# Prompt scores from three rounded products of high and low parts, in place of plain fp32

## The chip, the core and the metric

The kernel runs on one core of a Trainium2 chip. TensorE (PE) multiplies matrices out of SBUF into PSUM; VectorE (DVE), ScalarE (ACT) and GpSimd (POOL) do the rest of the arithmetic; SyncE (SP) and POOL issue most of the DMAs. The metric is the device time of one execution in microseconds (us), the median of several runs. Smaller is better.

## The reference

One step of a hybrid network with two layers over 640 tokens: a prompt of 512 frames and 8 running streams of 16 frames each. A layer is a half-step feed-forward block (FFN), a mixer (a short convolution, attention, and gates that merge them), and a second half-step FFN. The change lies in the attention of the prompt: 8 heads of 64 channels, 64-frame chunks, each of which reads its own chunk and those before it, and a learned bias by relative distance:

```python
s = jnp.einsum('bqhd,bkhd->bhqk', q, k).astype(jnp.float32) * (HEAD_DIM ** -0.5)
...
s = s + rel_bias[:, idx].astype(jnp.float32)[None]
...
valid = (k_pos[None, :] >= 0) & (kc <= qc) & (kc >= qc - N_PREV_CHUNKS)
s = jnp.where(valid[None, None], s, NEG_INF)
p = jax.nn.softmax(s, axis=-1).astype(v.dtype)
return jnp.einsum('bhqk,bkhd->bqhd', p, v)
```

All inputs and outputs are fp32. The keys of the prompt and of the streams are outputs too.

## The kernel before

**Rounded products.** Nearly all matrix products are done in a rounded fp32 form (type `fp32r`). A number z is split into hi, z rounded to that form by a copy on ScalarE, and lo = z - hi, a subtraction on VectorE that writes the same form. A product is then hi·hi + hi·lo + lo·hi, three matmuls into one PSUM bank. Weights are split so as well while they stream in: `raw` is loaded on SP's queue (L292), ScalarE writes `whi` (L364), VectorE `wlo` (L369).

**Seven products for eight.** A pair of output tiles (q and k of two heads, for example) is made by `seven` (L833), a Strassen-like scheme with seven half products on four chunks of weights. It is a generator: between its blocks of six matmuls it yields, 14 times in all. Banks pa, pb and pc (in the profile `ma_qk`, `mb_qk`, `mc_qk`) are read by VectorE and ScalarE in the middle of a pair and at its end; TensorE goes on adding to pa and pc after some of these readings. `both` (L1377) gives the readings for a pair without a convolution: `up1` and `up2` write the first output, `lo2` the second half (columns 320 to 639) of the second output, and `lo1` its first half (columns 0 to 319), last of all. `third` and `last` are called behind `up2` and `lo1`.

**Queries and keys.** `qk(p)` (L1796) makes q and k of heads 2p and 2p+1 as tiles of 128 channels (64 for each head) by 640 tokens. `queries`, run as `third`, scales q on VectorE (L1802) and copies the streams' part to `bd` on POOL; `keys`, run as `last`, stores k (L1809, a DMA that POOL issues) and copies the streams' part to `ks`. q and k have two buffers each, of the pool `mp` (tags "q" and "k").

**Filling.** TensorE's order is written out by hand through the attention: `fill(n)` takes n steps (blocks of six matmuls) of the stream `work` (q and k of pairs 1 to 3, then convolution, gates) and puts them between the parts of the attention, so that TensorE has work while softmax runs. `scores(p)` (L1859) does the scores of two heads, `turn(p)` transposes the weights, `values(p)` multiplies them with v. VectorE, ScalarE, POOL and SP have no order written out there: a planner orders their instructions by when it thinks that they can run, and those under `soon()` come ahead of others.

**Scores.** In `scores(p)` the prompt has four row blocks i of 128 queries, with 128·(i+1) keys each, so 128, 256, 384 and 512 columns. For each block the two heads come one behind the other: channels 0 to 63 and 64 to 127, into two different PSUM banks. These are fp32 matmuls (L1882). VectorE adds the bias and takes the maximum (L1888), ScalarE does the exponentials (L2082) and scales them (L1899).

**After the prompt.** The streams' attention reads cached keys (`kc`, L1992, loaded on SP's queue) into buffers of the tags "q" and "k", that is, into those that q and k of the prompt leave. `tmp` gives a tile of 128 x 640 out of four shared temporaries; the convolution uses two at a time.

## Time and profile before

| | |
|---|---|
| median of 3 runs | 2481.96 us (2481.89 to 2482.2) |
| the profiled execution | 2481.95 us |
| its span, first to last instruction | 2480.2 us |
| TensorE busy | 2467.0 us, 17264 matmuls |
| VectorE busy | 2182.4 us |
| ScalarE busy | 1385.6 us |
| granted TensorE clock | 1.0 |

How the lines are read: a row of a group has the line of the kernel, the engine, the operation, output tile <- input tiles (buffer numbers left out), shapes (partitions x elements), the count, and behind it the busy time in us and the mean of one in ns, then the idle time of the engine just before them and who ended it. A row of the timeline has start and length in us. A matmul's shape is given as rows x columns of the array, then the moving operand. An fp32 matmul shows as two matmuls; rounded operands are shown as f32 in matmul rows. A matmul's length covers its way through the array, so matmuls overlap, and the rate is the distance of their starts. PEld is the loading of weights into the array.

### The profile page before, as it was taken

How to read it: one execution, taken by the hardware profiler on the slowest of the kernel's cores; microseconds unless marked ns; L12 is line 12 of the kernel's file. 1: busy time of each engine (PE TensorE's matmuls, PEld its weight loads, DVE VectorE, ACT ScalarE, POOL GpSimd, SP SyncE). 2: the span in 40 equal slices, each digit the busy share in tenths (PEclk: the TensorE clock that was granted, in tenths of full speed). 3: DMA queues.
4: the chain of work that ended last, by engine and by line, in shares of the span. 5: the costliest groups of instructions: out<-in, count | busy, mean ns of one | idle time of the engine just before them, and what ended most of it. 6: DMA issues, size and time to landing. Idle time of an engine off the chain costs nothing.

```text
span 2480.2 us, 44054 instructions
## 1 busy us (share of the span) xinstructions
PE 2467.0 (99%) x17264; PEld 2414.6 (97%) x17264; DVE 2182.4 (88%) x3643; ACT 1385.6 (56%) x2230; POOL 319.5 (13%) x483
## 2 busy tenths in 40 slices
PE   9999999999999999999999999999999999999999
PEld 8999999889999999999999999998899999999998
DVE  7999998888888899998799999988888889999997
ACT  6555556675555555555665555566655556555555
POOL 0111112211000001111001010121110000111111
PEclk9999999999999999999999999999999999999999
DMA  4443444335344334444334343452453333444444
GB/s 155 127 117 102 120 118 125 110 114 174 99 118 124 94 102 107 112 118 118 110 94 109 110 117 102 117 128 103 137 167 94 118 119 93 107 113 107 112 117 117
DMA packets 113520, 288.16 MB, mean 116 GB/s; under 512 B 12992, under 2 KB 52544, under 8 KB 113312
## 3 DMA queue, kind: packets, MB, share of 16 engines
q1 hardware_dynamic: 69552, 220.10, 27.0%
q0 software_dynamic: 43328, 64.99, 13.8%
q8 instruction: 135, 2.21, 0.4%
q14 instruction: 73, 0.60, 0.1%
q10 hardware_dynamic: 432, 0.25, 0.0%
HBM read 239.48 MB, written 7.94 MB: 100 GB/s over the span
## 4 chain that ended last, share of the span: by engine, by line
PE 93%; DVE 3%; ACT 2%; issue 1%; DMA 1%; SPq 0%; DVEq 0%; ACTq 0%; POOLq 0%
PE pab L459 12%; PE paa L459 11%; PE pcb L459 6%; PE daa L1144 6%; PE pca L459 5%; PE dab L1144 5%; PE po L435 5%; PE qa L459 4%; PE pbb L459 3%; PE dca L1144 3%; PE pba L459 3%; PE dcb L1144 2%; PE ma_cv L459 2%; PE ma_qk L459 2%; PE py L435 2%; PE pv L1835 2%
## 5 line engine op out<-in xcount | busy, mean ns | idle before, releaser
L364 ACT CAST whi<-raw 128x512 fp32r<-128x512 f32 (+1 forms) x577 | 501.7, 874 | 371.6 <-PE pbb L459 46.0
L369 DVE TENSOR_TENSOR wlo<-raw,whi 128x512 fp32r<-128x512 f32 (+1 forms) x577 | 577.1, 1002 | 137.1 <-ACT whi L364 132.9
L364 ACT CAST whi<-s 128x1024 fp32r<-128x1024 f32 (+1 forms) x162 | 152.8, 943 | 320.3 <-DVE s L296 113.9
L459 PE MATMUL pab<-xhib,whi 128*128 128x320 f32 x704 | 217.7, 309 | 0.0
L459 PE MATMUL pab<-xlob,whi 128*128 128x320 f32 x704 | 217.3, 309 | 0.0
L459 PE MATMUL pab<-xhib,wlo 128*128 128x320 f32 x704 | 217.3, 309 | 0.0
L459 PE MATMUL paa<-xhia,whi 128*128 128x320 f32 x640 | 197.8, 309 | 0.2 <-DVE ga L296 0.2
L459 PE MATMUL paa<-xhia,wlo 128*128 128x320 f32 x640 | 197.6, 309 | 0.0
L459 PE MATMUL paa<-xloa,whi 128*128 128x320 f32 x640 | 197.5, 309 | 0.0
L369 DVE TENSOR_TENSOR wlo<-s,whi 128x1024 fp32r<-128x1024 f32 (+1 forms) x162 | 176.4, 1089 | 4.4 <-ACT whi L364 4.4
L1166 POOL DMA_DIRECT2D x<-c_a x80 | 69.8, 1019 | 575.2 <-ACT ahia L1048 205.5
L1166 POOL DMA_DIRECT2D x<-c_b x72 | 63.1, 1011 | 583.2 <-ACT ahib L1048 205.4
L459 PEld LDWEIGHTS pab<-xhib,whi 128*128 128x128 f32 x704 | 132.1, 188 | 0.9 <-issue 0.9
L459 PEld LDWEIGHTS pab<-xlob,whi 128*128 128x128 f32 x704 | 132.1, 188 | 0.0
L459 PEld LDWEIGHTS pab<-xhib,wlo 128*128 128x128 f32 x704 | 132.1, 188 | 0.0
L459 PEld LDWEIGHTS paa<-xhia,whi 128*128 128x128 f32 x640 | 120.1, 188 | 1.1 <-DVE ga L296 0.5
L459 PEld LDWEIGHTS paa<-xloa,whi 128*128 128x128 f32 x640 | 120.1, 188 | 0.3 <-DVE xloa L703 0.3
L459 PEld LDWEIGHTS paa<-xhia,wlo 128*128 128x128 f32 x640 | 120.1, 188 | 0.2
L296 DVE TENSOR_TENSOR raw<-s,raw 128x512 f32<-128x512 f32 x162 | 110.8, 684 | 0.0
L459 PE MATMUL pcb<-xhib,wlo 128*128 128x320 f32 x352 | 108.9, 309 | 0.0
L459 PE MATMUL pcb<-xlob,whi 128*128 128x320 f32 x352 | 108.7, 309 | 0.0
L459 PE MATMUL pcb<-xhib,whi 128*128 128x320 f32 x352 | 108.7, 309 | 0.0
(909 smaller groups left out, 8200.5 us busy)
## 6 DMA issues: line engine op xcount, KB each, us to landing
raw<-in_wst SPq DMA_DIRECT2D x375, 512.0 KB, 3.6
x<-c_a POOLq DMA_DIRECT2D x80, 160.0 KB, 4.9
x<-c_b POOLq DMA_DIRECT2D x72, 160.0 KB, 4.2
lent<-in_wst POOLq DMA_DIRECT2D x36, 256.0 KB, 3.7
kc<-in_kcache SPq DMA_DIRECT2D x32, 256.0 KB, 4.9
vc<-in_vcache SPq DMA_DIRECT2D x16, 512.0 KB, 4.3
one<-in_wst POOLq DMA_DIRECT2D x32, 256.0 KB, 3.9
x<-u_a POOLq DMA_DIRECT2D x40, 160.0 KB, 4.1
```

The lines of the kernel that those rows point to most:

```text
L296: DVE.tensor_tensor(out=out, in0=a, in1=b, op=op)
L364: ACT.copy(hi[:, d], src[:, c])
L369: DVE.tensor_tensor(out=lo, in0=src, in1=hi.bitcast(F32), op=ALU.subtract)
L435: PE.matmul(ps[:, a, :HT], w, x[a] if isinstance(x, tuple) else x[:, a * HT : (a + 1) * HT], start=first and j == 0 and not seeded, stop=l ...
L459: PE.matmul(ps, a, b, start=start and kp == 0 and j == 0, stop=stop and kp == NP - 1 and j == 2, skip_group_check=True)
L1144: PE.matmul(ps[u], w, y, start=start and i == 0 and j == 0, stop=i == 1 and j == 2, skip_group_check=True)
L1166: POOL.dma_start(x[ms[2 * u + r]][:, cols], z[:, u], accum_op=ALU.add)
L1835: PE.matmul(pv[t], xx[:, t * P : (t + 1) * P], w[:, kk * AW : (kk + 1) * AW], start=c == 0 and kk == 0 and j == 0, stop=c == KT // 2 - 1 a ...
```

## The change

q and k of the prompt are no longer kept as they are for the scores. They are made in two of the shared temporaries, and for each of them a high and a low part of the prompt's 512 columns are written into the two buffers that q (or k) had: `parts` does a ScalarE copy and a VectorE subtraction, both under `soon()`. q is split in one piece of 512 columns behind its scaling. k is split in two: columns 320 to 511 in the middle of the pair (through the new argument `mid` of `both`), columns 0 to 319 at its end.

In `scores` each block is three rounded products (high·high, low·high, high·low), added up in one bank, and for each of the three the heads alternate. The matmuls still use 64 rows for each head.

The calls of `fill` are changed so that every `scores(p)` comes one step later in TensorE's order; `turn` and `values` stay at the step where they were.

```diff
-                def both(n, u, g, third, last, scale=-1.0):
+                def both(n, u, g, third, last, scale=-1.0, mid=None):
 
                     (up1, up2), (lo2, lo1) = upper(u), lower(g, scale)
+
+                    def half(pa):
+                        lo2(pa)
+                        if mid:
+                            mid()
...
-                    return pair(n, up1, lo2, end1, end2)
+                    return pair(n, up1, half, end1, end2)
...
-            q = qa[p] = mp.tile([P, T], F32, name=f"q{l}_{p}", tag="q")
-            k = ka[p] = mp.tile([P, T], F32, name=f"k{l}_{p}", tag="k")
+            q = tmp(f"q{l}_{p}")
+            k = tmp(f"k{l}_{p}")
+            qa[p], ka[p] = ([mp.tile([P, T], F32R, name=f"{z}{i}{l}_{p}", tag=z)[:, :SEQ]
+                             for i in ("hi", "lo")] for z in "qk")
+
+            def parts(zs, z, c):
+                hi, lo = (y[:, c] for y in zs)
+                with soon():
+                    ACT.copy(hi, z[:, c])
+                    DVE.tensor_tensor(out=lo, in0=z[:, c], in1=hi.bitcast(F32), op=ALU.subtract)
 
             def queries():
                 DVE.scalar_tensor_tensor(out=q, in0=q, scalar=HD ** -0.5, in1=rr, op0=ALU.mult, op1=ALU.mult)
+                parts(qa[p], q, slice(0, SEQ))
...
             def keys():
+                parts(ka[p], k, slice(0, HT))
                 POOL.dma_start(ko[l, :, p, :], k)
                 POOL.tensor_copy(ks[:, p, :], k[:, SEQ:])
 
-            return both(f"qk{p}", q, k, queries, keys)
+            return both(f"qk{p}", q, k, queries, keys, mid=lambda: parts(ka[p], k, slice(HT, SEQ)))
...
+                (qh, ql), (kh, kl) = qa[p], ka[p]
                 for i, c in spans:
-                    for e in range(2):
-                        r = slice(e * HD, (e + 1) * HD)
-                        PE.matmul(pss[e][:, c], qa[p][r, i * P : (i + 1) * P], ka[p][r, : (i + 1) * P],
-                                  start=True, stop=True)
+                    for j, (y, z) in enumerate(((qh, kh), (ql, kh), (qh, kl))):
+                        for e in range(2):
+                            r = slice(e * HD, (e + 1) * HD)
+                            PE.matmul(pss[e][:, c], y[r, i * P : (i + 1) * P], z[r, : (i + 1) * P],
+                                      start=j == 0, stop=j == 2)
...
-        fill(2)
+        fill(3)
         scores(0)
         fill(15)
         scores(1)
-        fill(4)
+        fill(3)
         turn(0, 0)
         fill(2)
         turn(0, 1)
         fill(2)
         values(0)
-        fill(6)
+        fill(7)
         scores(2)
         for p in range(1, npair):
             if p + 1 < npair:
-                fill(6)
+                fill(5)
                 turn(p)
-                fill(8 if p + 2 < npair else 11)
+                fill(9 if p + 2 < npair else 11)
                 values(p)
```

## The prediction

> **What bounds the kernel now.** I read the page first, then what TensorE waited for, then the chain of work that ended last, and only then the lines of the change.
>
> ```profile
> span 2480.2 us, 44054 instructions
> ...
> PE 2467.0 (99%) x17264; PEld 2414.6 (97%) x17264; DVE 2182.4 (88%) x3643; ACT 1385.6 (56%) x2230; POOL 319.5 (13%) x483
> ```
>
> ```profile
> PE poa L435 <- ACT whi L759: 5.3, 1, 5.3
> PE pca L459 <- DVE wlo L369: 0.5, 2, 0.3
> ```
>
> The profiled execution took 2481.95 us: its span of 2480.2 and 1.75 us around it. The median of the runs is 2481.96, so a sum against the profiled execution needs no correction. TensorE (PE) is busy for 99% of the span. Its longest wait in the whole kernel is the 5.3 us at the start, and no row of that list after the second is above 0.5. For the stretch from 440 to 560 us, which holds the attention of the first layer, the list is empty. So a microsecond taken off TensorE's own stream shows at the end, and work on VectorE (DVE) or ScalarE (ACT) costs nothing until TensorE has to wait for it.
>
> From the chain (start, length, what):
>
> ```profile
> 428.53 13.62 PE pv L1835 x60
> ...
> 471.48 2.36 PE pss L1882 x16
> ...
> 477.55 1.76 PE mc_qk L459 x12
> ...
> 514.80 2.18 PE ptp L1919 x20
> ...
> 2455.98 5.92 PE pdf L2197 x48
> ```
>
> and from the line of the scores:
>
> ```profile
> L1882 PE MATMUL pss<-k,q x128: 269/429/693, 471.4 to 1756.5; 64*128 64x512 f32 x32, 64*128 64x256 f32 x32, 64*128 64x128 f32 x32, 64*128 64x384 f32 x32
> ```
>
> The scores of one pair of heads (pss) are 16 matmuls in 2.36 us, and 128 / 16 makes eight such calls, four in each layer: 18.9 us in all. This is everything that the change can shorten, under 0.8% of the time.
>
> **Part 1: the products of the scores.** The 16 matmuls are two passes for each of eight fp32 products (four widths, two heads). From four narrow stretches of the first call, a row of each, and below them the loads of weights:
>
> ```profile
> 471.41 0.70 PE L1882 MATMUL pss<-k,q 64*128 64x512 f32 x2
> 471.94 1.03 PE L1882 MATMUL pss<-k,q 64*128 64x512 f32 x6
> 472.37 0.82 PE L1882 MATMUL pss<-k,q 64*128 64x256 f32 x8
> 472.80 1.03 PE L1882 MATMUL pss<-k,q 64*128 64x128 f32 x8
> ```
>
> ```profile
> 471.41 0.30 PEld L1882 LDWEIGHTS pss<-k,q 64*128 64x128 f32 x4 [0.19 <-issue]
> ```
>
> Two matmuls of up to 0.69 us lie within 0.70 from 471.41: the two heads already run beside each other, each in its 64 rows. The second pass over 512 columns lasts from 471.94 to 472.37, 0.43 us, and two passes over 256 from 472.37 to 472.80, 0.215 each. A pass moves 1.2 columns per ns, so a pair needs 2 x 1280 / 1.2 = 2.13 us; the other 0.23 of the 2.36 goes into changing to this mode and back (0.10 of it is seen in the first pass, which takes from 471.41 to 471.94).
>
> After the change each width has three rounded products. Rates of rounded products stand in the chain: 13.62 / 60 = 0.227 us for 512 columns, 1.76 / 12 = 0.147 for 320, 5.92 / 48 = 0.123 for 256. From 320 to 512 a column costs 0.42 ns, so 384 columns cost 0.174. For 128 rounded columns there is no row. Below, the line from 320 through 256 goes on to 0.075; above, the transposes of that width take 2.18 / 20 = 0.109. I take 0.109, the one row of that width. With the heads beside each other a pair costs 3 x (0.227 + 0.123 + 0.109 + 0.174) = 1.90 us, with the lower bound 1.80. That rounded halves run beside each other as the fp32 ones do is taken from these; no row shows it. The other end is one after the other, 3.80.
>
> Whether the 0.23 stays has no row either, since every small tile here is also fp32 and type and tile change together. Its bounds are 0 and 0.23; I keep 0.23, as the nearest row is this call's own. The new call is 1.90 + 0.23 = 2.13 in place of 2.36: 0.23 less, **1.9 us less in eight calls**. The Trainium skill, TensorEngine Tiling (Array Packing), Key Properties, says that changing the tiling mode drains the engine; by it the 0.23 stays, without it the call would be 1.90.
>
> The four loads of weights at 471.41 end within 0.30 us, while the first two matmuls run until 472.11. The third and fourth are for the same two halves, so a load goes on beside a matmul of its own half. The Trainium skill, TensorE: Matmul & The Clock Gate, The mechanism (Part 3), says that a load overlaps a matmul in flight only where the row group differs. The trace disagrees, for fp32; if it held for rounded products it would be the rival "loads" below.
>
> **Part 2: the rounded parts.** Each pair gets three copies on ScalarE (512, 320 and 192 columns) and three subtractions of these widths on VectorE.
>
> ```profile
> L369 DVE TENSOR_TENSOR wlo<-s,whi 128x512 fp32r<-128x512 f32 x6 | 4.2, 701 | 0.0
> ...
> L1368 DVE SCALAR_TENSOR_TENSOR k<-ma_qk,rrm 128x320 f32<-128x320 f32 x4 | 1.9, 484 | 0.0
> ```
>
> ```profile
> L364 ACT CAST whi<-s 128x512 fp32r<-128x512 f32 x6 | 3.7, 615 | 5.9 <-DVE s L296 5.8
> ...
> L863 ACT COPY c<-mc_qk 128x320 f32<-128x320 f32 x4 | 1.6, 412 | 0.0
> ```
>
> Busy time of PE, PEld, DVE, ACT, POOL in the whole attention of the first layer, and in one pair's stretch of it:
>
> ```profile
> 457.26:558.27 101.01, 101.01 (x701) 90.11 (x699) 81.99 (x193) 69.03 (x158) 17.16 (x42) 1.00 0.37 126
> ```
>
> ```profile
> 469.56:484.42 14.86, 14.86 (x102) 13.54 (x101) 12.37 (x34) 10.76 (x25) 3.11 (x8) 1.00 0.37 130
> ```
>
> With the 320 price as the upper end for 192, VectorE gets 0.70 + 0.48 + 0.48 = 1.66 us a pair and ScalarE 0.62 + 0.41 + 0.41 = 1.44; in eight pairs 13.3 and 11.5. In the 101.01 us VectorE is idle for 19.0 and ScalarE for 32.0, and four pairs need 6.6 and 5.8. In the pair's own stretch VectorE has 2.49 idle for its 1.66. The cover is TensorE's filling products, and on average it holds: cost 0. Were it gone, VectorE's 13.3 us would show.
>
> The average isn't all. A subtraction waits for its copy at the head of VectorE's queue; behind it stand the weights' subtractions, the taking out of the next banks, and the maxima of the softmax, on which TensorE waits. Two places are tight:
>
> ```profile
> 469.61 0.82 DVE L1802 SCALAR_TENSOR_TENSOR q<-q,rrm 128x640 f32<-128x640 f32 x1
> 470.35 0.48 DVE L1368 SCALAR_TENSOR_TENSOR k<-ma_qk,rrm 128x320 f32<-128x320 f32 x1
> ...
> 480.87 1.23 DVE L369 TENSOR_TENSOR wlo<-raw,whi 128x1024 fp32r<-128x1024 f32 x1 [2.49 <-ACT whi L364]
> 482.02 0.17 DVE L2085 RECIPROCAL st<-st 128x4 f32<-128x4 f32 x1
> 482.10 0.46 DVE L296 TENSOR_TENSOR k<-ma_qk,c 128x320 f32<-128x320 f32 x1
> ```
>
> ```profile
> 482.66 0.38 PE L459 MATMUL ma_qk<-thi,whi 128*128 128x320 f32 x1
> 482.87 0.31 PE L459 MATMUL ma_qk<-tlo,whi 128*128 128x320 f32 x1
> ```
>
> First, the start of the scores. Now q is ready at 470.43, k at 470.83, and the scores begin at 471.41. One filling step is half of the 1.76 us of twelve products, 0.88, so they would begin at 472.29. New in between: ScalarE copies q until 471.05 and k until 471.46; VectorE subtracts q until 471.75 and k until 472.23. k's low part is needed only after two products of 512 columns, 0.45 later. So the first call has about 0.5 us in hand, and the other three of a layer, which now have a step more, 0.88 more. Cost 0; one foreign operation of 0.62 or 0.70 us in front would use it up in the first call.
>
> Second, the product after a bank's middle reading. At 482.10 VectorE takes out k's half, behind a weight subtraction that itself waited 2.49 us for ScalarE, and TensorE's next product on that bank starts when it is done (482.66, 0.38 long in place of 0.31). There is nothing in hand there. ScalarE's softmax now comes 0.88 us later against the filling products and its queue is 1.44 us fuller, so this can get later or, with another order, earlier. Bounds: a gain of the 0.1 us that it costs now, a loss of one 512-column subtraction, 0.70, in each pair. I take 0.1 us more for each of the eight pairs, near the row, **0.8 us**.
>
> **Part 3: what moves with the scores and the tiles.** The scores, with the bias loads that POOL issues for the pair after, come one step later, and all later fills are adjusted so that transposes and values keep their places. Issue and need of a bias shift together: cost 0. q and k now live in the four shared temporaries; the convolution's tiles that follow take the buffers of pair 2, whose outgoing DMA is a whole pair (14 steps of 0.88) back: cost 0. Both buffers of a name now hold the high and low part of one pair, so the cached keys of the first sample batch, loaded on SP's queue into the same buffers, can start only when the last scores are done:
>
> ```profile
> 509.43 0.39 SPq L1992 DMA_DIRECT2D kc<-in_kcache  x1
> ...
> 528.85 0.38 SPq L1992 DMA_DIRECT2D kc<-in_kcache  x1
> ```
>
> ```profile
> L2005 PE MATMUL spss<-kc,bd x128: 392/392/417, 558.3 to 1839.5; 128*32 128x272 f32 x128
> ```
>
> They go from 509.43 to about 528.85 with the second batch's, and are first used at 558.3: cost 0. Weight loads stand on the same queue; if the order of that queue weren't adjusted, one of them would wait up to 19 us. POOL's copy of the new keys into these tiles waits for the same release.
>
> **Sum.** 2481.95 - 1.9 + 0.8 = 2480.85; I predict 2480.8.
>
> **The rivals.**
> - *The switch goes too.* If the 0.23 belongs to fp32 and not to the small tile, and 128 columns cost 0.075, a call is 1.80: 0.56 less, and the product behind it also loses its late start, about 0.1 by the 0.10 at the entry. 8 x 0.66 = 5.3 us: 2476.7. For it: no row separates type and tile. Against: it needs both bounds at once. With one of them it is 2478 to 2480.
> - *The queues get in the way.* One 0.70 us subtraction in front of TensorE in each pair: 2481.95 - 1.9 + 5.6 = 2485.7; a 1024-column one of 1.23 us: 2489.9. It decides once VectorE runs later than the 0.5 us in hand at the scores or the nothing at 482.66. For it: that row, and ScalarE 1.44 us fuller. Against: 19.0 us of idle in 101.
> - *Loads.* Every product pays for its load. A load of 128 columns is at most the 0.109 of a transpose; twelve a call, in front of their products: 1.80 + 12 x 0.109 + 0.23 = 3.34, 0.98 more, 2489.8. Against: the row of four loads. Nearly the same time comes out if a rounded 64-row tile runs no faster than fp32, so that the change doesn't do what it says: 3 x 1280 / 1.2 + 0.23 = 3.43, 2490.5.
> - *One head after the other.* 3.80 + 0.23 = 4.03 a call, 1.67 more: 2495.3. It decides if a rounded product holds all 128 rows. For it: no rounded product of 64 rows is in the trace. Against: the two fp32 halves at 471.41.
>
> **How the numbers follow.** Forecast 47%, its own range 2479 to 2482.5; the switch 18%; the queues 16%; loads or no faster 8%; one after the other (or a blocked weight load) 11%. About 0.2% is what a measurement of this kernel can tell from no change: below 2477.0 is faster, above 2486.9 slower. Faster holds 15 of the switch's 18; slower holds 9 of the queues', 8 and 11: 28; the rest, 57, is same. The range from 2476.5 to 2490 leaves out the last rival and a little at both ends.
>
> **What would show it.** A score call in the chain of 24 matmuls and about 2.13 us; two matmuls from one moment in its first stretch; three intervals near 0.23 us for 512 columns. Near 1.8 the switch went; near 3.4 it is loads or rate; near 4 the heads follow each other. Waits of TensorE for the new high and low parts, or longer first products behind a bank's reading, would show the queues. The prediction is wrong if pss rows keep 2.36 us or more with TensorE still at 99%.

## The result, and the profile after

The changed kernel takes **2487.64 us** (median of 13 runs, 2486.96 to 2488.61) against 2482.2 (median of 13 runs beside it, 2481.72 to 2482.68): a ratio of **1.0022, with an interval of 1.0013 to 1.003**. It is slower by 5.4 us where 1.2 us less was forecast. The profiled execution took 2488.61 us.

From the page of the changed kernel, its span, the busy times, and the shares by engine of the chain that ended last:

```profile
span 2486.8 us, 44241 instructions
...
PE 2468.2 (99%) x17328; PEld 2418.0 (97%) x17328; DVE 2192.3 (88%) x3667; ACT 1393.8 (56%) x2254; POOL 313.2 (13%) x483
...
PE 89%; DVE 5%; ACT 3%; issue 1%; DMA 1%; SPq 0%; DVEq 0%; ACTq 0%; POOLq 0%
```

TensorE is still busy for 99% of the span, and on the first two lines nothing seems to have happened. But the chain, of which 93% had been TensorE, is now 89% TensorE, with VectorE grown from 3% to 5% and ScalarE from 2% to 3%. The list of TensorE's waits in the whole kernel tells where (total, times, longest):

```profile
PE poa L435 <- ACT whi L759: 5.5, 1, 5.5
PE ma_cv L459 <- ACT capsm L859: 1.5, 2, 0.8
PE mc_qk L459 <- ACT c L863: 1.1, 2, 0.6
PE qa L459 <- ACT capsm L1525: 1.0, 1, 1.0
PE pca L459 <- DVE wlo L369: 0.5, 2, 0.3
PE ma_cv L459 <- DVE yc L296: 0.5, 2, 0.3
PE ma_qk L459 <- ACT capsm L859: 0.5, 2, 0.2
PE ma_qk L459 <- DVE k L296: 0.4, 2, 0.2
```

Before, only the first and the fifth of these were there. The new ones with "2" for the times are one in each layer, all on *filling* products (`ma_`, `mc_`) whose bank ScalarE or VectorE has yet to read. None is a product of the scores. (The single 1.0 us at `qa` lies outside the attention. Such a wait turns up in some of the profiled executions below and not in others; it is about the 0.97 us by which this execution lies above the median.)

The loss can be measured more finely than by the time of the whole. I take the stretch from the first product of pair 0 (`ma_qk`) to the first product of the streams' scores (`spss`): in both kernels it holds the same 492 filling products, 80 transposes, four score calls and four value calls. Rows of the windows' view, with length first and then the busy times of PE, PEld, DVE, ACT and POOL; the first two are the second layer before and after, the last the first layer after (the first layer before is quoted in the prediction):

```profile
1685.49:1786.50 101.01, 101.01 (x702) 90.11 (x700) 81.92 (x193) 69.02 (x158) 16.79 (x42) 1.00 0.37 126
```

```profile
1689.47:1793.10 103.63, 101.52 (x733) 91.99 (x731) 87.21 (x205) 72.94 (x170) 17.06 (x44) 1.00 0.36 123
...
457.37:561.02 103.65, 101.53 (x734) 91.99 (x732) 87.24 (x205) 72.94 (x170) 17.96 (x44) 1.00 0.35 123
```

The stretch grew by 2.64 and 2.62 us, 5.3 in both layers, which is the 5.4 of the medians. What follows didn't change: from there to the first product of the tile `qa` it is 77.26 us in both profiles. In all kernels below the two layers of this stretch agree within 0.17 us, mostly within 0.05, where the interval of a ratio of times is some 4 us wide; so the smaller differences are read here from the stretch. The exception is e8, whose profiled execution ran at a granted clock of 0.16 from 942 us on, so that only its first layer is read.

The scores themselves did become shorter. TensorE's timeline of the second call after:

```profile
488.61 0.50 PE L1899 MATMUL pss<-khi,qhi 64*128 64x512 f32 x2
488.95 0.39 PE L1899 MATMUL pss<-khi,qlo 64*128 64x512 f32 x2
489.18 0.40 PE L1899 MATMUL pss<-klo,qhi 64*128 64x512 f32 x2
489.41 0.28 PE L1899 MATMUL pss<-khi,qhi 64*128 64x256 f32 x2
...
489.76 0.22 PE L1899 MATMUL pss<-khi,qhi 64*128 64x128 f32 x2
...
490.44 0.33 PE L1899 MATMUL pss<-klo,qhi 64*128 64x384 f32 x2
490.71 0.41 PE L459 MATMUL ma_qk<-thi,whi 128*128 128x320 f32 x1
```

Each row is two matmuls, one for each head, and 490.71 - 488.61 = 2.10 us is the call, in place of 2.36. The four calls of the layer, read in this way, are 2.30, 2.10, 2.10 and 2.51, 9.01 in place of 9.44. The first and the last hold waits: the first 0.2 us, at its third product, which starts at 473.06, just behind the subtraction that writes k's low part until 473.00; the last 0.4, of which 0.3 for a bank that the values' copy `ya` reads until 529.70. So the scores gave 0.4 us a layer and the filling products between them took 3.1: by the distances of their starts they need 77.04 us in place of 73.98. The list of waits has only 2.0 us a layer for the filling. It counts a wait from the end of the product in front, and a product is 0.31 long at a distance of 0.147; counted by starts, each wait is longer.

### The profile page after: what moved, and what is told of

Read it like the earlier page. It is cut to its first block, busy times and chain, and to the rows that moved or that the text cites. A ratio compares the mean times of both kernels' runs of the same rounds, so it can differ in the third digit from the quotient of the medians.

```text
span 2486.8 us, 44241 instructions
## 1 busy us (share of the span) xinstructions
PE 2468.2 (99%) x17328; PEld 2418.0 (97%) x17328; DVE 2192.3 (88%) x3667; ACT 1393.8 (56%) x2254; POOL 313.2 (13%) x483
## 4 chain that ended last, share of the span: by engine, by line
PE 89%; DVE 5%; ACT 3%; issue 1%; DMA 1%; SPq 0%; DVEq 0%; ACTq 0%; POOLq 0%
PE pab L459 12%; PE paa L459 11%; PE pcb L459 6%; PE daa L1144 6%; PE pca L459 5%; PE dab L1144 5%; PE po L435 5%; PE qa L459 4%; PE pbb L459 3%; PE dca L1144 3%; PE pba L459 3%; PE dcb L1144 2%; PE py L435 2%; PE pv L1850 2%; PE ma_cv L459 2%; PE qc L459 2%
## 5 line engine op out<-in xcount | busy, mean ns | idle before, releaser
L364 ACT CAST whi<-raw 128x512 fp32r<-128x512 f32 (+1 forms) x577 | 501.6, 874 | 358.9 <-PE pbb L459 47.3
L364 ACT CAST whi<-s 128x1024 fp32r<-128x1024 f32 (+1 forms) x162 | 152.8, 943 | 315.3 <-issue 111.3
```

What stands on the lines that cost most here:

```text
L364: ACT.copy(hi[:, d], src[:, c])
```

## The experiments

Two theories stood against each other at first: that the scores come at the wrong place of TensorE's order (the shift of one step alone), and that the new copies and subtractions get in the way on ScalarE and VectorE. For each kernel the table has the stretch in the first layer, in it the filling products and the score calls, and the time with its ratio to the kernel before beside it. Where an expectation or a diff names a base, it is the kernel after, if not told otherwise.

| kernel | stretch | filling | scores | time, us | ratio |
|---|---|---|---|---|---|
| before | 101.01 | 73.98 | 9.44 | 2482.2 | |
| after | 103.65 | 77.04 | 9.01 | 2487.64 | 1.0013 to 1.003 |
| e1 | 102.13 | 75.09 | 9.44 | 2484.8 | 1.0002 to 1.002 |
| e2 | 104.57 | 77.25 | 9.72 | 2489.21 | 1.0018 to 1.0041 |
| e3 | 103.31 | 76.57 | 9.14 | 2486.68 | 1.0009 to 1.0027 |
| e4 | 103.54 | 75.81 | 10.14 | 2487.78 | 1.0014 to 1.0032 |
| e5 | 101.39 | 75.33 | 8.41 | 2483.44 | 0.9996 to 1.0015 |
| e6 | 107.16 | 79.23 | 10.07 | 2495.66 | 1.0037 to 1.0073 |
| e7 | 108.00 | 75.74 | 14.67 | 2496.09 | 1.004 to 1.0072 |
| e9 | 102.97 | 75.94 | 9.44 | 2486.03 | 1.0007 to 1.0025 |
| e10 | 103.23 | 76.55 | 9.09 | 2486.67 | 1.001 to 1.0029 |
| e11 | 100.99 | 73.95 | 9.44 | 2482.19 | 0.9991 to 1.001 |
| e12 | 102.22 | 76.24 | 8.45 | 2484.27 | 1.0 to 1.0019 |
| e13 | 102.64 | 75.52 | 9.44 | 2486.04 | 1.0007 to 1.0026 |
| e14 | 100.68 | 74.71 | 8.43 | 2481.6 | 0.999 to 1.0008 |
| e15 | 102.03 | 76.06 | 8.43 | 2485.09 | 1.0003 to 1.0022 |
| e16 | 101.70 | 75.75 | 8.41 | 2483.46 | 0.9997 to 1.0016 |
| e17 | 103.76 | 75.94 | 10.23 | 2487.62 | 1.0013 to 1.0032 |
| e18 | 101.22 | 75.27 | 8.41 | 2482.62 | 0.9995 to 1.0013 |

**The places: e1, e2, e3.** e1 is the kernel before with the changed `fill` calls and nothing else.

```diff
-        fill(2)
+        fill(3)
         scores(0)
...
-        fill(4)
+        fill(3)
         turn(0, 0)
...
-        fill(6)
+        fill(7)
         scores(2)
...
-                fill(6)
+                fill(5)
                 turn(p)
-                fill(8 if p + 2 < npair else 11)
+                fill(9 if p + 2 < npair else 11)
```

> The kernel before with the fills of the kernel after: fp32 scores, no parts, every scores call one step later. Theory 'shift' (the later scores leave one filling step less until a bank that ScalarE still has to copy out is needed, and that copy stands behind the softmax): the waits of 0.4 to 0.9 us behind scores 0 to 3 appear here too, some 3 us a layer, 2487 to 2489 us. Rival 'parts' (the new copies and subtractions fill the queues): no such waits, 2482.2 within 0.7.

The shift alone lengthens the stretch by 1.12 us and the time by 2.7. A part of it is the very place that the prediction called tight. Rows of e1's timeline, VectorE first, then the product that waits for it:

```profile
481.78 1.23 DVE L369 TENSOR_TENSOR wlo<-raw,whi 128x1024 fp32r<-128x1024 f32 x1 [2.22 <-ACT whi L364]
483.01 0.46 DVE L296 TENSOR_TENSOR k<-ma_qk,c 128x320 f32<-128x320 f32 x1
```

```profile
483.52 0.41 PE L459 MATMUL ma_qk<-thi,whi 128*128 128x320 f32 x1 [0.30 <-DVE k L296]
```

The same two VectorE instructions stand in the same order as before. Counted from the start of the stretch, k's reading is 0.56 us later (483.01 - 457.61 = 25.40, before 482.10 - 457.26 = 24.84), since the scores that feed ScalarE are 0.88 later; and as there was nothing in hand, the product is 0.51 later too (25.91 in place of 25.40).

e2 keeps the change and gives it back the places of before; e3 shifts the first scores only.

```diff
-        fill(3)
+        fill(2)
         scores(0)
...
-        fill(3)
+        fill(4)
         turn(0, 0)
...
-        fill(7)
+        fill(6)
         scores(2)
...
-                fill(5)
+                fill(6)
                 turn(p)
-                fill(9 if p + 2 < npair else 11)
+                fill(8 if p + 2 < npair else 11)
```

> The kernel after with the fills of before: rounded products and parts, no scores call moved. 'Shift': the waits behind scores 1 to 3 go; the gain of the products, 1.9 us, shows, less up to 1 us a layer where the first scores now come too early for their low parts: 2480 to 2482. 'Parts': the waits stay, 2487 to 2489.

```diff
-        fill(15)
+        fill(14)
         scores(1)
-        fill(3)
+        fill(4)
         turn(0, 0)
...
-        fill(7)
+        fill(6)
         scores(2)
...
-                fill(5)
+                fill(6)
                 turn(p)
-                fill(9 if p + 2 < npair else 11)
+                fill(8 if p + 2 < npair else 11)
```

> The kernel after with only the first scores call one step later, the others where they were before. 'Shift': as with the old fills, without the wait of the first call, 2480 to 2481.5. 'Parts': 2487 to 2489.

With its old places the change costs 3.56 us a layer. From e2's list of waits in the whole kernel:

```profile
PE ma_cv L459 <- ACT capsm L859: 1.9, 2, 0.9
PE pss L1899 <- DVE qlo L1812: 0.8, 4, 0.2
PE pss L1899 <- ACT khi L1811: 0.8, 2, 0.4
```

Here the scores wait for the parts, and most of this is gone once they come later; but the longest wait is again on a filling product. So the shift does help the new scores (103.65 against 104.57) and hurts the old ones (102.13 against 101.01). e3, with only the first scores moved, is 0.34 below the kernel after. No choice among these three places brings the loss below 2.3 us a layer, so the move by one step isn't the main cause; places further back follow below.

**The parts: e4, e5, e9.** e4 makes the parts and leaves them unread; the products are fp32 as before. e9 makes only the copies. e5 reads rounded products, without the low parts.

```diff
+            full[p] = q, k
...
-                (qh, ql), (kh, kl) = qa[p], ka[p]
                 for i, c in spans:
-                    for j, (y, z) in enumerate(((qh, kh), (ql, kh), (qh, kl))):
-                        for e in range(2):
-                            r = slice(e * HD, (e + 1) * HD)
-                            PE.matmul(pss[e][:, c], y[r, i * P : (i + 1) * P], z[r, : (i + 1) * P],
-                                      start=j == 0, stop=j == 2)
+                    for e in range(2):
+                        r = slice(e * HD, (e + 1) * HD)
+                        PE.matmul(pss[e][:, c], full[p][0][r, i * P : (i + 1) * P], full[p][1][r, : (i + 1) * P],
+                                  start=True, stop=True)
```

> The kernel after with plain fp32 products of q and k in the scores; the high and low parts are made but not read, the fills are those of after. Both theories: the products' own gain is missing, 1.9 us above the kernel after, about 2489.5; if the rounded products gain nothing, 2487.6.

e9 is e4 with one line less:

```diff
                     ACT.copy(hi, z[:, c])
-                    DVE.tensor_tensor(out=lo, in0=z[:, c], in1=hi.bitcast(F32), op=ALU.subtract)
```

> The kernel after with ScalarE's copies of the high parts kept but not read, no subtractions, and plain fp32 products in the scores. Beside the kernel without low parts (stretch 101.39 us, rounded products) it gives the products' price while VectorE carries no subtraction. Theory 'given back' (the products gain their 1.04 us a layer, and with VectorE late it turns into waits): stretch 102.2 to 102.6, time about 2484.7 to 2485.5. Rival 'no gain' (the products' shorter calls never count): stretch 101.4, time 2483.4.

and e5 is the kernel after without that line, and with

```diff
-                    for j, (y, z) in enumerate(((qh, kh), (ql, kh), (qh, kl))):
+                    for j, (y, z) in enumerate(((qh, kh),) * 3):
```

> The kernel after without the low parts: the six subtractions of a pair's q and k... three on VectorE for each pair are left out, and the three products all take the high parts. Left out: the low parts, so the scores are only rounded ones. ScalarE's copies, the matmul count and the fills stay. Theory 'VectorE' (the subtractions make VectorE late, the maxima and so the exponentials and the copies behind them): the attention stretch falls from 103.65 us to that of the moved fills less the products' gain, 102.1 - 1.0 = 101.1, and the time to about 2482.5. Theory 'ScalarE' (the copies do it): the stretch stays within 0.5 of 103.65 and the time above 2486.5.

The rows of the stretches of e4 and e5 in the first layer:

```profile
457.71:561.25 103.54, 102.55 (x702) 90.42 (x700) 86.79 (x205) 72.83 (x170) 19.05 (x44) 1.00 0.37 123
```

```profile
457.19:558.58 101.39, 100.87 (x734) 91.78 (x732) 82.57 (x193) 72.77 (x170) 19.51 (x44) 1.00 0.36 126
```

With e1 these make a path from before to after in single steps: shift +1.12 (e1), copies +0.84 (e9), subtractions +0.57 (e4), rounded products +0.11 (after). The last number is the surprise: products that are 0.25 us a call shorter bring nothing. Between e4 and after, the score calls do fall by 1.13 us (10.14 to 9.01), and the filling products rise by 1.23 (75.81 to 77.04). TensorE gets through its scores sooner and then waits by as much for banks which VectorE and ScalarE haven't read. By the other path, shift, copies, rounded products, subtractions, the steps are +1.12, +0.84, **-1.58** (e5 against e9) and **+2.26** (after against e5). So the products are worth what was forecast (0.95 us a layer) as long as the subtractions aren't there: the score calls fall by 1.03 (9.44 to 8.41). The rest of the 1.58 is filling (75.94 to 75.33), where an order of two instructions comes back, as the next rows show. And the subtractions, 4.7 us of VectorE's time in a layer (87.24 - 82.57), cost 2.26 us once TensorE goes faster, although VectorE is idle for 16.4 of the 103.65 us.

One of these waits shows how ScalarE takes part. Behind the last transposes of pair 0, ScalarE has two instructions: the reading of the bank `mc_qk` (L863) and a cast of weights (L364). Rows of its timeline, before:

```profile
497.60 0.41 ACT L863 COPY c<-mc_qk 128x320 f32<-128x320 f32 x1
497.90 1.06 ACT L364 CAST whi<-raw 128x1024 fp32r<-128x1024 f32 x1
```

The reading ends at 498.01 and the product that needs it starts at 498.06: there was nothing in hand. After, with the product that needs the reading:

```profile
497.57 1.04 ACT L364 CAST whi<-raw 128x1024 fp32r<-128x1024 f32 x1
498.51 0.42 ACT L863 COPY c<-mc_qk 128x320 f32<-128x320 f32 x1
...
498.98 0.41 PE L459 MATMUL mc_qk<-hhim,whi 128*128 128x320 f32 x1 [0.55 <-ACT c L863]
```

The cast has gone ahead of the reading, and TensorE waits 0.55 us for it. In e1 and e5 the reading is first, and no wait of this kind is listed. In e9 the cast is first, the wait is 0.8 us, and the six filling products in front of it take 1.93 us in place of e1's 1.06: that is about the whole 0.84 which the copies cost. After, the six take 1.68, in e5 1.07: 0.61 of the 2.26 above is this one order again. This is a price of the order, not of how full ScalarE is (it is busy 72.98 of 102.97 us in e9 and 72.77 of 101.39 in e5). ScalarE doesn't go on with a later instruction while an earlier one waits: in the rows below it stands idle until 534.48, although the bank that it copies at 534.88 was finished at 532.83. Why the planner, which makes this order, came to another one in these two kernels was not looked into.

The other kind of wait is a chain through both engines, at the fourth call of scores. VectorE after:

```profile
525.45 0.48 DVE L1812 TENSOR_TENSOR klo<-k,khi 128x320 fp32r<-128x320 f32 x1
...
527.46 0.68 DVE L296 TENSOR_TENSOR raw<-s,raw 128x512 f32<-128x512 f32 x1
529.25 1.23 DVE L369 TENSOR_TENSOR wlo<-raw,whi 128x1024 fp32r<-128x1024 f32 x1 [1.11 <-ACT whi L364]
530.40 0.68 DVE L1905 CUSTOM_DVE_ANT_0 s<-pss,bias 128x512 f32<-128x512 f32 x1
```

ScalarE and TensorE after:

```profile
528.17 1.05 ACT L364 CAST whi<-raw 128x1024 fp32r<-128x1024 f32 x1 [1.40 <-DVE raw L296]
...
534.48 0.40 ACT L2099 ACTIVATE s<-s,st 128x128 f32<-128x128 f32 x1 [4.26 <-DVE st L2097]
...
534.88 0.40 ACT L859 COPY capsm<-ma_cv 128x320 f32<-128x320 f32 x1
```

```profile
528.29 0.50 PE L1899 MATMUL pss<-khi,qhi 64*128 64x512 f32 x2
...
535.34 0.42 PE L459 MATMUL ma_cv<-thi,whi 128*128 128x320 f32 x1 [0.76 <-ACT capsm L859]
```

and the same instructions before, TensorE's, then ScalarE's:

```profile
526.31 2.43 PE L1882 MATMUL pss<-k,q 64*128 64x512 f32 x16
...
533.17 0.31 PE L459 MATMUL ma_cv<-thi,whi 128*128 128x320 f32 x1
```

```profile
532.57 0.40 ACT L859 COPY capsm<-ma_cv 128x320 f32<-128x320 f32 x1
```

Before, the bank copy `capsm` ended at 532.97, and the product that needs it came at 533.17: 0.2 us in hand, and so no wait that any list could show. After, the copy starts 6.59 us behind the start of the scores (534.88 - 528.29) in place of 6.26 (532.57 - 526.31). The product, which came 6.86 behind it (533.17 - 526.31), would now come 6.13 behind it: a filling step of 0.88 earlier, since the scores moved and the filling did not, and 0.15 later for the longer call (2.51 in place of 2.36). The copy's end at 6.99 is 0.86 too late for that, and the product starts 0.92 behind 6.13 (535.34 - 528.29 = 7.05). Of what went missing the move took 0.88 and the longer chain 0.33, against the 0.20 in hand and the 0.15 of the longer call. Further up: the copy stands behind the softmax's first exponential, this waits 4.26 us for the maxima, the maxima stand on VectorE behind a weight subtraction, which waits 1.11 us for its cast on ScalarE, and the cast for a VectorE sum (`raw`, 527.46), which stands behind the low parts of k and q. While ScalarE is idle for 4.26 us and VectorE for 1.11, TensorE loses 0.76: every engine has idle time, and the chain through their queues has none.

**GpSimd for the parts: e6, e7.** If VectorE's or ScalarE's time was the price, an idle engine could take it.

```diff
-                    ACT.copy(hi, z[:, c])
+                    POOL.tensor_copy(hi, z[:, c])
```

> The kernel after with the high parts copied by POOL in place of ScalarE. 'ScalarE': the copies' 1.44 us a pair leave the queue that TensorE waits for, stretch below 102.5, time 2483 to 2485. 'VectorE': stretch 103 to 104 or longer, since POOL's copies are slower and the subtractions wait for them at the head of VectorE's queue; time 2487 to 2491.

```diff
-                    DVE.tensor_tensor(out=lo, in0=z[:, c], in1=hi.bitcast(F32), op=ALU.subtract)
+                    POOL.tensor_tensor(out=lo, in0=z[:, c], in1=hi.bitcast(F32), op=ALU.subtract)
```

> The kernel after with the low parts subtracted by POOL in place of VectorE. 'VectorE': stretch 101.1 to 102.3 and time 2482.5 to 2485, unless the scores then wait for POOL's slower subtraction, which would show as waits of pss. 'ScalarE': stretch about 103.6, time 2487 to 2488.

They are slower than the change by 3.5 and 4.4 us a layer. The line of q's subtraction in e7 (durations min/median/max in ns), then in the kernel after and in e6, and e7's waits in the whole kernel:

```profile
L1812 POOL TENSOR_TENSOR qlo<-q,qhi x8: 1628/1693/1712, 472.9 to 1766.3; 128x512 fp32r<-128x512 f32 x8
```

```profile
L1812 DVE TENSOR_TENSOR qlo<-q,qhi x8: 678/679/775, 471.8 to 1756.9; 128x512 fp32r<-128x512 f32 x8
```

```profile
L1812 DVE TENSOR_TENSOR qlo<-q,qhi x8: 1169/1172/1174, 472.5 to 1761.9; 128x512 fp32r<-128x512 f32 x8
```

```profile
PE pss L1899 <- POOL klo L1812: 3.8, 6, 0.8
PE pss L1899 <- POOL qlo L1812: 3.7, 4, 1.4
```

In e6 it isn't GpSimd's copies that are slow: they take 0.61 us for 512 columns, as ScalarE's do after. But VectorE's subtraction of q, with GpSimd copying beside it, takes 1.17 us in place of 0.68, and VectorE is busy for 90.23 us of the stretch in place of 87.24. ScalarE is busy 4.3 us less (68.61 in place of 72.94), and yet TensorE's wait at `mc_qk` for ScalarE's reading grows from 1.1 to 2.3 us in the whole kernel. So taking work off ScalarE didn't shorten TensorE's waits for it, here beside a slower VectorE.

In e7 GpSimd needs 1.69 us where VectorE needs 0.68, and the scores wait for it. Beside these waits the filling products of e7 take 75.74 us, 1.30 less than after (0.97 in the second layer): with the subtractions off VectorE's queue that part of the loss goes, or TensorE is held up at the scores long enough to hide it. e7 can't tell these two apart.

**Less work on VectorE elsewhere: e10 and e11.** Of every four weight subtractions in the attention, the last goes to GpSimd; e10 does it to the kernel after, e11 to the kernel before as a control.

```diff
-            pending.append((lo[:, d], src[:, c], hi[:, d]))
+            pending.append((POOL if spare[0] and slabs[i][0] == "mix" and slabs[i][2] == 3 else DVE,
+                            lo[:, d], src[:, c], hi[:, d]))
...
-        for lo, src, hi in pending:
-            DVE.tensor_tensor(out=lo, in0=src, in1=hi.bitcast(F32), op=ALU.subtract)
+        for on, lo, src, hi in pending:
+            on.tensor_tensor(out=lo, in0=src, in1=hi.bitcast(F32), op=ALU.subtract)
```

> The kernel after with one weight subtraction of each pair's four chunks (the last, 512 columns) done by POOL in place of VectorE during the attention. It takes 0.6 us of unrelated work a pair from VectorE and touches no part of the scores. Theory 'load of VectorE': the waits shrink by a good part, stretch 101.5 to 103, time 2482 to 2486. Rival 'the low parts themselves are late': stretch 103.6, time 2487.6.

> The kernel before with the same weight subtractions on POOL, as the control: it has no waits to lose in the attention, so the stretch stays at 101.01 and the time at 2482 within 0.7; if POOL is too slow for these weights, both rise.

The control costs nothing in the stretch (100.99), so nothing there waits for these instructions on GpSimd; and on the change this gives back 0.42 of the 2.64 us, with VectorE 1.47 us less busy (85.77 in place of 87.24). The 0.42 is what is left of two opposite shifts: TensorE's waits in the whole kernel for `capsm` at `ma_cv` fall from 1.5 to 0.2 us, as the chain shown above gets shorter, and those at `mc_qk` rise from 1.1 to 1.7. For each us of work on VectorE this is 0.29 us of the stretch, where the low parts cost 0.48 on one path (2.26 / 4.67) and 0.14 on the other (0.57 / 4.00, e4 against e9): there is no one price for VectorE's load.

**Scores much later: e8, e12 to e16.** If the parts and the queues need time, scores further back might have it. e8 puts them behind the sixth step of the next pair.

```diff
-        fill(3)
+        fill(6)
         scores(0)
-        fill(15)
+        fill(14)
         scores(1)
...
-        for p in range(1, npair):
...
+        fill(5)
+        turn(1)
+        fill(7)
+        values(1)
+        fill(2)
+        scores(3)
+        fill(4)
+        turn(2)
+        fill(11)
+        values(2)
+        fill(2)
+        turn(3)
+        fill(6)
+        values(3)
```

> The kernel after with each scores call behind the sixth step of the next pair, that is behind the product whose bank ScalarE copies out, and with the transposes moved along. If the cost comes from that copy standing behind exponentials that wait for the maxima, the 0.4 to 1.1 us waits for it go: stretch 101 to 102, time 2480 to 2484. If only the load of the queues counts, waits of the same sum show up elsewhere: stretch 103 or more, time 2486 or more.

e8 took 2490.5 us (median of four executions; a ratio of 1.0021 to 1.0051). It also moved the last values three steps back, so that its stretch of 104.60 us holds three filling steps (2.64) more and the streams' part three less, which still took 78.01 us in place of 77.26: TensorE waited there. It doesn't answer the question. e12 has the same places for the scores, and the last values at the step where they were.

```diff
+        fill(4)
+        turn(1)
+        fill(8)
+        values(1)
+        fill(2)
+        scores(3)
+        fill(4)
+        turn(2)
+        fill(9)
+        values(2)
+        fill(1)
+        turn(3)
+        fill(6)
+        values(3)
```

> The kernel after with the scores behind the sixth step as in the run with later scores, but with the last values at the same step as before, so that the streams' part begins where it did. If the waits for ScalarE's copy behind the exponentials go and nothing takes their place: stretch 101 to 102, time 2480.5 to 2484. If VectorE's load decides: other waits, stretch 102 to 104, time 2484 to 2488.

e13 is the kernel before with these `fill` calls, e14 is e12 without the low parts, made as e5 was:

> The kernel before with the later places of the last run (scores behind the sixth step of the next pair, same end): fp32 products, no parts. Theory 'place' (a scores call a step later left too little time for the bank's copy, six steps later leaves enough): stretch 101.0 to 101.4, time 2482 to 2483. If any move of the scores costs: stretch 102 or more.

> The later places without the low parts (left out: the low parts; the three products all take the high parts). If the subtractions are what is left of the cost there: stretch 100.0 to 100.6 (the products' 1.04 us shows), time 2480 to 2481.5. If the copies or the place cost: 101 to 102.

e15 is e12 with the edit of e10, e16 is e15 with one subtraction of k (columns 320 to 511) on GpSimd too:

```diff
-                    DVE.tensor_tensor(out=lo, in0=z[:, c], in1=hi.bitcast(F32), op=ALU.subtract)
+                    (POOL if c.start else DVE).tensor_tensor(out=lo, in0=z[:, c], in1=hi.bitcast(F32), op=ALU.subtract)
```

> The later places, rounded products with all parts, and one weight subtraction of four on POOL. 'Load of VectorE': the waits that are left (0.3 to 0.7 us for VectorE's results) shrink, stretch 100.5 to 101.8, time 2481 to 2483.5. If only the order in the queues decides: stretch as without it, 102.2, time 2484.

> As the run before, with the subtraction of k's columns 320 to 511 on POOL too (it has some four steps until the scores). 'Load of VectorE': a further 0.1 to 0.4 us a layer less, 2480.5 to 2483. 'Order': no steady change.

The stretch of e14 in the first layer, in which TensorE is busy but for 0.15 us:

```profile
458.02:558.70 100.68, 100.53 (x733) 91.91 (x732) 82.58 (x193) 73.06 (x170) 17.62 (x44) 1.00 0.36 127
```

The three steps again, at other places: the place alone +1.63 (e13 against before), copies and rounded products together -1.96 (e14), subtractions +1.54 (e12). The same order of sizes as above, with 2.26 for the subtractions there: they cost at both places, and the size depends on the place. All score calls are 2.09 to 2.12 in e12 and e14, so no score waits, and e12 is 1.43 us a layer better than the change. Relief by GpSimd brings another 0.2 (e15), and with k's subtraction 0.5 in all (e16); the times can't show steps so small, and that of e15 lies 0.8 us above e12's. Of the kernels with rounded scores e14 is the only one with a shorter stretch than the kernel before, by 0.33 us; in time it can't be told from it, and it leaves the low parts out.

**The order alone: e17 and e18.** So far each edit had also changed the order in the queues. These two change nothing else: the readings of banks in `seven` get a higher priority with the planner, in e17 at the places of the change, in e18 at those of e12.

```diff
-        with soon():
+        with tc.high_priority(offset=900):
             ACT.copy(c1, pa)
...
-        with soon():
+        with tc.high_priority(offset=900):
             ACT.copy(c5, pc)
...
-        with soon():
+        with tc.high_priority(offset=900):
             third(pc)
```

(and so for all seven readings)

> The kernel after, but the readings of the banks in a pair of tiles (on ScalarE and VectorE) get a higher priority with the planner, 900 in place of 300; no instruction is added or removed. In the queue of ScalarE the reading of mc_qk then stands ahead of the weight cast behind pair 0's last transposes, as in the kernel before. If the loss comes from the order of single instructions in the queues, the wait of 0.6 us there and most of those for capsm go, and the stretch falls by 1 us or more a layer, to 102.6 or less, the time to some 2485.5. If it is the length of the chain or the work on VectorE as such, the stretch stays within 0.4 us of 103.65 and the time near 2487, as other instructions then come late in place of these.

> The scores at the later places of e12, and the readings of banks ahead in the order as in e17. If the order is what is left of the loss there, the stretch falls from 102.22 to 101.2 or less and the time to 2482.5 or below, level with the kernel before; if it is the chain or the work, it stays within 0.4 us of 102.2 and the time near 2484.

From e17's waits in the whole kernel:

```profile
PE ma_cv L459 <- ACT capsm L859: 1.5, 2, 0.8
PE ma_qk L459 <- ACT capsm L859: 1.3, 2, 0.6
PE pss L1899 <- DVE qlo L1812: 0.9, 2, 0.4
PE pss L1899 <- ACT ya L1971: 0.8, 2, 0.4
```

The wait at `mc_qk` is gone, as meant: the reading stands ahead of its cast again, and the six products in front of it take 0.97 us. The filling products take 75.94 us, 1.10 less than after. But the scores take 10.23, 1.22 more, and wait for q's low part and for a bank that the values' copy `ya` leaves: what was put back in the queue is now what TensorE waits for, and the stretch stays at 103.76. At these places the loss isn't the order of these readings alone; in either order something that TensorE needs comes late.

At the later places it is mostly the order: e18's stretch is 101.22, 1.00 below e12's, which was 1.21 above the kernel before, and the scores take 8.41. Of e12's two waits inside the attention one is left:

```profile
PE ma_qk L459 <- DVE wlo L369: 0.7, 2, 0.4
```

e18 takes 2482.62 us against 2482.0 beside it, a ratio of 0.9995 to 1.0013. It is the best kernel found with the change's computation: level with the kernel before and not better, since its filling products still take 1.29 us a layer more than there, and the scores 1.03 less.

## Why the prediction was wrong, point by point

**Part 1, the products: right in its size.** It took 2.13 us for a call, made of intervals of 0.227, 0.123, 0.109 and 0.174 and a switch of 0.23. An undisturbed call takes 2.10: 0.23 between the 512-column products, 0.34 for the first of them (0.11 of it the entry), and 0.27 behind the last, where 0.174 was due (0.10 the way out). The switch stayed, 0.21 of 0.23. The Trainium skill, TensorEngine Tiling (Array Packing), Key Properties, says that a change of tiling mode drains the engine; the rows agree, with this 0.21 inside a call. Two matmuls from one moment in every row: *One head after the other* fell. *Loads* fell too; the timeline of the loads in that call:

```profile
488.71 0.19 PEld L1899 LDWEIGHTS pss<-khi,qlo 64*128 64x128 f32 x2
488.95 0.19 PEld L1899 LDWEIGHTS pss<-klo,qhi 64*128 64x128 f32 x2
```

The weights of the second product are loaded from 488.71, in the same two halves in which the first runs until 489.11 (488.61 + 0.50), and the third's from 488.95. The rule of TensorE: Matmul & The Clock Gate, The mechanism (Part 3), of the Trainium skill, that a load overlaps only with another row group, isn't borne out by rounded products either.

**The step from there to the end.** "A microsecond taken off TensorE's own stream shows at the end" was read from the kernel before, whose stretch has no listed wait; no run shortens TensorE's stream there and changes nothing else. It fits e5, where the calls bring 1.03 us and the stretch falls by 1.58 (against e9). At the change's places with the subtractions in VectorE's queue it fails: 1.13 us off the scores, 1.23 us on to the filling (after against e4).

**Part 2, the parts: the failed term.** The forecast put them at 0.8 us, all of it at the product behind a bank's middle reading, and at 0 elsewhere, since on average VectorE had 19.0 us idle for 6.6 and ScalarE 32.0 for 5.8. Copies and subtractions cost 0.84 + 0.57 us a layer with fp32 products and, on the other path, 0.84 + 2.26: 2.8 or 6.2 us in both layers, in place of 0.8. In the terms of the sum: the score calls gave 0.9 us in both layers where 1.9 was put, and the filling products took 6.1 more where 0.8 was put for the parts and 0 for the move. The averages were even on the safe side (VectorE is busy 5.25 us more in the stretch, ScalarE 3.9) and proved nothing. The forecast saw that a subtraction stands in front of the maxima, called two places tight, and still sized the tight one by 0.1 us, "near the row". It overlooked that a product which doesn't wait may be 0.2 us from waiting, as `ma_cv` at 533.17 was; a list of waits that is empty shows no margins. At the named place, 482.10 before, the kernel after has no wait at all: the reading ends at 482.97, and the product starts at 483.24, 0.147 behind the one in front. The same kind of reading in a later pair costs 0.2 us a layer (`ma_qk` behind `k`). The largest waits were at the readings of `ma_cv` and `mc_qk` by ScalarE, which the forecast didn't name. At the first scores the 0.5 us in hand was used up by what the forecast itself had named, one foreign operation: a weight subtraction of 0.67 us at 471.23 stands in front of q's, and the call has its 0.2 us of waits. The second and third calls have none, as forecast.

**Part 3, the moved scores: 0 was wrong too, in both directions.** Alone the move costs 1.12 us a layer (e1); with the change made, it gains 0.92 (after against e2), 0.71 of it in the scores (9.72 to 9.01), which then wait less for their parts. The forecast moved the scores' own needs (biases, buffers, keys) with them, and there it was right: no wait of TensorE for a buffer of q and k, a bias load or the cached keys appears (the 0.3 us in the fourth call are for a bank of the scores). But the softmax behind the scores also reads banks of the filling products in the same queues, and these had not moved.

**The rivals.** *The queues get in the way* is what happened, by its mechanism and at 2487.64 between its two prices, 2485.7 and 2489.9; its 16% was too little. The sign that the forecast gave for it, longer first products behind a bank's reading, is what the rows show. Its place was wrong: it put one VectorE instruction in front of TensorE in each pair, and the runs show several shorter waits, on ScalarE's readings above all. *The switch goes too* fell, as it stayed.

**What stays open.** The single steps don't add up in one way, since each edit also changes the planner's order; e17 and e18 show the share of one order among many: nothing at the change's places, 1.0 us a layer at the later ones. An order of ScalarE and VectorE written out by hand through the attention, which might bring e18's 101.22 down to the 100.0 that the shorter scores allow (101.01 - 1.03), wasn't tried.

## What to carry to other kernels

Where one engine is fed through in-order queues of two others, idle time on average is no cover: look, for every product that reads or reuses a bank, at how long before it the reading ended, and price an added instruction against the smallest of these margins. Moving one part of a hand-written order moves everything that stands behind it in the other engines' queues; try the move alone before the change that needs it. And a saving on the bound engine counts only as far as the chain through the others lets it arrive earlier: add the edits by two paths, since here the same products were worth 1.58 us a layer on one path, part of it an order that came back, and nothing on the other.

## What the runs showed of the hardware

- Rounded products of 64 rows run two at a time, at the same distance as those of 128 rows: 0.23 us for 512 columns (488.95 to 489.18), 0.12 for 256 (three from 489.41 to 489.76). From the first of 128 columns to the last of 384 it is 0.68 (489.76 to 490.44), as the forecast's 3 x 0.109 + 2 x 0.174 gives; the last one's own distance can't be told from the way out.
- GpSimd subtracts 512 columns of fp32 into the rounded form in 1.69 us where it makes q's low part (e7) and in 1.30 where it makes weights' (median, e11), VectorE in 0.68: at 1.9 to 2.5 times VectorE's it was no help for anything that TensorE needs within a step or two, and a harmless place for what it doesn't (e11). A copy of 512 columns takes 0.61 on GpSimd (e6) as on ScalarE (after).
- VectorE can be slower beside work on GpSimd: all eight of q's subtractions took 1.17 us where GpSimd did the copies (e6), in place of 0.68.
- The switch into 64-row tiles and back has a part outside the call as well: the first product of a call starts 0.24 us behind the last one of 128 rows (488.37 to 488.61), and the second product behind the call 0.25 us after the first (490.71 to 490.96), both in place of 0.147. It is the same before the change (0.24 and 0.25), so it doesn't enter the comparison.
